# Own buffers for raw weights and adaLN tiles, a moved split at the mixer's start, and three merge buffers

## The chip, the cores and the metric

The kernel runs on one NeuronCore of a Trainium2 chip. The metric is the time of one execution on the device in microseconds. The names of the engines: PE is the matrix engine (TensorE), DVE the vector engine, ACT the scalar engine, POOL the GpSimd engine, SP the engine that issues most DMA transfers; "SPq" and "ACTq" are the rows of transfers issued by SP and ACT. Every engine works through its own instructions in the order in which they stand in the program and waits for the others by semaphores.

## What is computed

One layer of an encoder on a sequence of 512 tokens with 1024 channels, in float32:

```
mod = silu(c) @ w_ada + b_ada                  # 9 x 1024: shift, scale, gate of three blocks
h = h + 0.5 * g1 * FFN1(modulate(rmsnorm(h)))  # (silu(u @ Wa) * (u @ Wb)) @ w_down, inner size 2816
h = h +       g2 * Mixer(modulate(rmsnorm(h)))
h = h + 0.5 * g3 * FFN2(modulate(rmsnorm(h)))
out = rmsnorm(h)
```

The mixer multiplies by `w_in` (q, k, v, gates), runs a short convolution, a bidirectional chunked delta rule over 8 heads and a gated short-convolution branch. It projects both branches (`w_b_out` is the kernel's `w_bo`), merges them as sigmoid(gate_A)\*A + sigmoid(gate_B)\*B and multiplies by `w_out` (`w_o`). The adaLN product `silu(c) @ w_ada` is a matrix-vector product; its matrix has 72 tiles of 128 x 1024.

## The kernel before

**The products.** Activations lie transposed, channels on the 128 partitions and 512 tokens in the free dimension. A float32 product is made of three products of a reduced type: the weight is split into `hi` (a cast on ACT) and `lo` (a subtraction on DVE), the activation likewise into `uh`/`ul` or `g` hi/lo, and for each k-tile PE makes hi\*hi, lo\*hi and hi\*lo (lines 209, 210 and 211).

**A weight's way** (`weight`, lines 188 to 200). A raw tile of 128 x 1024 (512 KB; 128 x 768 for the third part of a down row) comes by one DMA from SP into the pool `wraw`, which has three buffers (L192). ACT casts it in halves of four k-tiles (L197), DVE subtracts (L199), and the halves lie in the pool `wsp` with three buffers for hi and three for lo. SP works in order: where a raw tile has no free buffer, SP stands, with all later transfers behind it. The scheduler gives the steps of a weight a priority that puts them ahead of their place in the code (`tc.high_priority(WOFF)`), and so orders each engine's instructions before the run.

**An adaLN tile** (`ada`, L172 and L173) is a raw tile of `w_ada` that DVE multiplies by the replicated activation and sums along the row; PE has no part in it. DVE works in order too: while it stands at an adaLN tile that has not arrived, the `lo` subtractions behind it wait. Tiles 0 to 15 come at the start, 16 to 31 during the last up products of FFN1, in buffers of `wraw`; 32 to 63 during FFN1's down product, in four slices of a tile named `room` that takes the place of FFN1's `uh`; and 64 to 71 during FFN2's down product, again in `wraw`. `spread` and `gate_along` hook them into the loops of products.

**The stages** (times of the profiled execution): start to 65 us; FFN1's up products to 251, with a fast form (fewer products, L406) from 107 to 206.5; FFN1's down product to 378, seven rows m of three weights each (the weight number n = 3m + i, 0 to 20) and the row m = 7 in two halves of 256 tokens; the mixer's projections and delta rule to 885; the merge to 930; `w_o` to 970; FFN2's up products to about 1205 and its down product to 1330.

**The mixer's start.** So that PE has work while FFN1's last half closes, the first three weights of `w_in`, numbers 12, 20 and 28, are split ahead into a pool `mlead` of six buffers, and are used in two halves of 256 tokens. `uh`(m) are the modulated inputs, made by ACT and DVE for each m and half. `sq` are the squares for the norm, `rs` the reciprocal root.

**The merge** (L1055 to 1080). For each of eight m, the gates' logits `msa` and `msb` and the first branch `mpa` come from DRAM by DMA from ACT's queue, ACT makes the sigmoids, DVE multiplies and adds, and the sum is split to `mh` and `ml`, the input of `w_o`. These tiles have two buffers each in the pool `mw`.

Of the kernel before, what the change touches and what calls it, by code (L numbers as in the profile page):

```python
# [16 lines left out]
P = 128  # L17
# [49 lines left out]
def tile_layer(  # L67
# [33 lines left out]
    wsp = open_pool(ctx, "wsp", bufs=3)  # L101
    upool = open_pool(ctx, "upool")
    sm = {}
    lead = {}
    psum = open_pool(ctx, "psum", bufs=ACC, space=PSUM)
    psx = open_pool(ctx, "psx", bufs=1, space=PSUM)
    psum_ch = open_pool(ctx, "psum_ch", bufs=CH, space=PSUM)
# [77 lines left out]
        dve.tensor_scalar(out=g, in0=g, scalar1=0.5, scalar2=None, op0=ALU.mult)  # L185


    def weight(src, nk, sp=None):
        sp = sp or wsp
        with tc.high_priority(WOFF):  # L190
            raw = wraw.tile([P, nk, P], F32, tag="raw", name="raw")
            nc.sync.dma_start(raw[:], src)  # L192
            parts = []
            for k in range(0, nk, 4):
                n = min(4, nk - k)
                hi = sp.tile([P, n, P], F32R, tag="hi", name="hi")
                act.copy(hi[:], raw[:, k : k + n, :])  # L197
                lo = sp.tile([P, n, P], F32R, tag="lo", name="lo")
                dve.tensor_sub(lo[:], raw[:, k : k + n, :], hi[:].bitcast(F32))  # L199
                parts.append((hi, lo))  # L200
        return parts
# [12 lines left out]
    def product(*args):  # L214
        for _ in product_steps(*args):
            pass
# [55 lines left out]

    HALVES = ((0, T // 2, "kq"), (T // 2, T, "o"))

    def residual(ws, rhs, gate, h, res, ssum, after, hp=0, tail=1, hook=None):

        def close(m, ps, r, t0, t1):
            dve.scalar_tensor_tensor(out=h[:, m, t0:t1], in0=ps[:, t0:t1], scalar=gate[:, m : m + 1],  # L280
                                     in1=r[:, t0:t1], op0=ALU.mult, op1=ALU.add)
            square_in(ssum, h[:, m, t0:t1], m, t0, t1)

        for m in range(KT - tail):
            ps, r = bank(), res(m)
            for i, (w, k0, nk, first, last) in enumerate(ws(m)):
                product(ps, weight(w, nk), rhs, k0, nk, first, last)
                if hook:
                    hook(3 * m + i)
# [22 lines left out]
    def ffn(st, u, big, hd, wu, wd, gate0, ssum, after, fast, early=None, hook=None, hook2=None, hp=0, base=0,  # L312
            up_done=None, comb=None, save=None):
        gp = open_pool(st, "gp")
        tp = open_pool(st, "ftp", bufs=2)
        T2 = T // 2
# [143 lines left out]
        for j in range(FT):  # L460
            if j == fast.start - 1:

                lead["st"].close()
                fp = open_pool(fst, "fast", side="right")
            if j == fast.start and full:
                put(0, x, *place[0])
            if j == fast.stop:
                part(4)
                fst.close()
                new_lead()  # L470
            if j in fast:
                i = 2 * j - ne + base
                split(hi[:, j, :], lo[:, j, :], seven(i, i + 1, fp)[:])
                continue
            ps = []
            for s in range(2):
                i = 2 * j + s - ne
                if i < 0:
                    ps.append(early[i])
                    continue  # L480
                ps.append(bank())
                product(ps[-1], weight(wu[i + base], KT), u, 0, KT, True, True)
                if hook:
                    hook(n)
                n += 1
            sa = tp.tile([P, T], F32, tag="sa", name="sa")
            act.activation(out=sa[:], in_=ps[0][:], func=ACT.Silu)
            dve.tensor_mul(sa[:], sa[:], ps[1][:])
            split(hi[:, j, :], lo[:, j, :], sa[:])
        if up_done:  # L490
            up_done()
        if full:
            fst.close()
            new_lead()
            ssum[:] = new_sums()
        h = big.tile([P, KT, T], F32, tag="big", name="h")

        def res(m):
# [2 lines left out]
            return r  # L501

        residual(lambda m: [(wd[m, :, k0 : k0 + nk, :], k0, nk, k0 == 0, k0 == 16) for k0, nk in ((0, 8), (8, 8), (16, 6))],
                 (hi, lo), mod[:, gate0 : gate0 + KT], h, res, ssum, lambda *t: after(h, *t), hp, hook=hook2)
        return h


    def mixer(st, u, h, post):
# [26 lines left out]
        with ExitStack() as dd:  # L535
# [14 lines left out]
            split(bw[:, :, 0:32], bw[:, :, 32:64], raw[:])  # L550
            sel = dt.tile([64, 32], F32, name="sel")
            dve.tensor_add(sel[:], ident[0:64, 0:32], ident[0:64, 32:64])
            lp = open_pool(dd, "mlead", bufs=6)
            ew = {i: weight(w_in[i], KT, lp) for i in (12, 20, 28)}
            ps = bank("ch", psum_ch)

            def early_half(t0, t1):
# [491 lines left out]
        with ExitStack() as mg:  # L1049
# [97 lines left out]
    csd = kept.tile([P, D], F32, name="csd")  # L1147
    h2d = kept.tile([P, KT, T], F32, name="h2d")

    def spread(a, b, j0, j1, then, bufs=None):  # L1150

        def hook(j):
            if j0 <= j < j1:
                for n in range(a + (b - a) * (j - j0) // (j1 - j0), a + (b - a) * (j + 1 - j0) // (j1 - j0)):
                    ada(n, raw=bufs and bufs[n % 4])
                    if n == 23:
                        modulation(16, 24)
                        mod_gate(0)
                if j == j1 - 1:
                    then()  # L1160
        return hook
# [4 lines left out]
        mod_scale(1)  # L1166
        mod_scale(2)

    u1 = u
    def room():  # L1170

        x = upool.tile([P, 4, D], F32, tag="uh", name="room")
        ada_bufs.extend(x[:, i, :] for i in range(4))
        u2.extend(new_u())

    u2, ada_bufs = [], []
    with ExitStack() as st:

        n = 2 * FAST1.start - E8
        h = ffn(st, u1, big, xT, w1u, w1d, 16, ssum, lambda h, *t: modulated(u2, h, 1, *t), FAST1, early,  # L1180
                spread(*ADA[0], n, 2 * (FT - len(FAST1)) - E8, lambda: None),
                spread(*ADA[1], 0, M1, mixer_ready, ada_bufs), up_done=room, comb=comb)
    lead["st"].close()
    first.close()
    with ExitStack() as st:
# [11 lines left out]
    with ExitStack() as st:  # L1197
# [78 lines left out]
```

## Time and profile before

| | us |
|---|---|
| median of 3 runs | 1346.35 (1344.49 to 1347.13) |
| profiled execution, its own time | 1341.37 |
| its span, first to last instruction | 1339.4 |
| PE busy | 1305.7 (97%) |
| DVE busy | 962.0 (72%) |
| ACT busy | 639.5 (48%) |
| granted clock, mean | 0.997 |

Lines of the profile read as follows. A group: line, engine, operation, out<-in, count, then busy time in us, the mean ns of one, and behind the bar the idle time before them with what ended most of it. A wait: engine and line, what it waited for, total us, times, the longest. A window: its stretch and length, busy us of PE, PEld, DVE, ACT and POOL (with counts), granted clock of PE (1.00 is full), share of the DMA engines, GB/s. A timeline row: start, duration, engine, line, operation; in brackets the idle time before and what ended it.

### The profile page before, as it was taken

How to read it: one execution, taken by the hardware profiler on the slowest of the kernel's cores; microseconds unless marked ns; L12 is line 12 of the kernel's file. 1: busy time of each engine (PE TensorE's matmuls, PEld its weight loads, DVE VectorE, ACT ScalarE, POOL GpSimd, SP SyncE). 2: the span in 40 equal slices, each digit the busy share in tenths (PEclk: the TensorE clock that was granted, in tenths of full speed). 3: DMA queues.
4: the chain of work that ended last, by engine and by line, in shares of the span. 5: the costliest groups of instructions: out<-in, count | busy, mean ns of one | idle time of the engine just before them, and what ended most of it. 6: DMA issues, size and time to landing. Idle time of an engine off the chain costs nothing.

```text
span 1339.4 us, 22097 instructions
## 1 busy us (share of the span) xinstructions
PE 1305.7 (97%) x8471; PEld 1132.9 (85%) x8471; DVE 962.0 (72%) x1983; ACT 639.5 (48%) x1299; POOL 64.6 (5%) x103
## 2 busy tenths in 40 slices
PE   8999999999999999999999999999999999999997
PEld 6889998777888888787777787887899999997886
DVE  7968887678367979776856784647688888884443
ACT  4445563222247773566464334545445556552230
POOL 0000000000010110112012001000000000000000
PEclk9999999999999999999999999999999999999999
DMA  9533336898433443344333242567523323335441
GB/s 349 173 110 111 111 124 205 286 339 286 143 130 104 149 147 118 100 139 130 111 111 117 73 142 80 187 198 245 187 111 110 111 95 109 112 116 169 140 127 63
DMA packets 83026, 199.91 MB, mean 149 GB/s; under 512 B 25129, under 2 KB 27369, under 8 KB 82666
## 3 DMA queue, kind: packets, MB, share of 16 engines
q1 hardware_dynamic: 64984, 164.29, 37.6%
q10 hardware_dynamic: 17938, 34.23, 7.4%
q8 instruction: 66, 1.08, 0.3%
q14 instruction: 38, 0.31, 0.1%
HBM read 175.39 MB, written 23.10 MB: 148 GB/s over the span
## 4 chain that ended last, share of the span: by engine, by line
PE 63%; DMA 12%; issue 10%; DVE 8%; ACT 4%; POOL 2%; SPq 0%; ACTq 0%; POOLq 0%; DVEq 0%
PE acc L406 11%; PE acc L211 11%; PE acc L210 10%; PE acc L209 10%; PE ch L406 8%; DMA room<-w_ada 3%; DVE lo L199 2%; DMA raw<-w_ada 2%; DMA msb<-gtd 2%; PE acc L1135 1%; ACT hi L197 1%; DMA raw<-w2u 1%; PE ch L872 1%; PE ch L1135 1%; PE o L895 1%
## 5 line engine op out<-in xcount | busy, mean ns | idle before, releaser
L197 ACT CAST hi<-raw 128x512 fp32r<-128x512 f32 (+1 forms) x304 | 181.7, 608 | 300.9 <-PE acc L211 245.0
L209 PE MATMUL acc<-uh,hi 128*128 128x512 f32 (+1 forms) x776 | 298.4, 386 | 3.8 <-ACT hi L197 2.3
L210 PE MATMUL acc<-uh,lo 128*128 128x512 f32 (+1 forms) x776 | 297.2, 384 | 0.4 <-DVE lo L199 0.3
L211 PE MATMUL acc<-ul,hi 128*128 128x512 f32 (+1 forms) x776 | 295.7, 383 | 0.0
L199 DVE TENSOR_TENSOR lo<-raw,hi 128x512 fp32r<-128x512 f32 (+1 forms) x304 | 202.5, 675 | 128.4 <-ACT hi L197 127.0
L209 PEld LDWEIGHTS acc<-uh,hi 128*128 128x128 f32 x776 | 146.9, 189 | 28.1 <-ACT hi L197 2.3
L210 PEld LDWEIGHTS acc<-uh,lo 128*128 128x128 f32 x776 | 146.8, 189 | 24.0 <-DVE lo L199 0.8
L211 PEld LDWEIGHTS acc<-ul,hi 128*128 128x128 f32 x776 | 146.2, 189 | 24.1
L210 PE MATMUL acc<-g,lo 128*128 128x512 f32 (+1 forms) x396 | 145.3, 367 | 3.4 <-DVE lo L199 3.4
L209 PE MATMUL acc<-g,hi 128*128 128x512 f32 (+1 forms) x396 | 145.1, 366 | 1.1 <-ACT hi L197 1.1
L211 PE MATMUL acc<-g,hi 128*128 128x512 f32 (+1 forms) x396 | 144.5, 365 | 0.0
L210 PEld LDWEIGHTS acc<-g,lo 128*128 128x128 f32 x396 | 74.4, 188 | 17.4 <-DVE lo L199 5.6
L209 PEld LDWEIGHTS acc<-g,hi 128*128 128x128 f32 x396 | 74.4, 188 | 13.6 <-ACT hi L197 1.5
L211 PEld LDWEIGHTS acc<-g,hi 128*128 128x128 f32 x396 | 74.4, 188 | 11.9
L406 PE MATMUL acc<-dh,hi 128*128 128x256 f32 x368 | 80.4, 282 | 0.2 <-ACT sa L414 0.2
L634 DVE SCALAR_TENSOR_TENSOR cacc<-acc,cvd_sb,cacc 128x510 f32<-128x510 f32 (+1 forms) x96 | 70.9, 742 | 3.2 <-ACT cacc L629 2.6
L220 DVE TENSOR_TENSOR lw<-raw,hw 128x1024 fp32r<-128x1024 f32 x42 | 51.4, 1224 | 28.8 <-ACT hw L219 28.2
L219 ACT CAST hi<-s 128x512 fp32r<-128x512 f32 x84 | 52.0, 620 | 36.5 <-PE ch L406 14.2
L219 ACT CAST hw<-raw 128x1024 fp32r<-128x1024 f32 x42 | 44.0, 1049 | 48.7 <-PE acc L406 27.7
L406 PE MATMUL acc<-dh,lo 128*128 128x256 f32 x224 | 63.3, 283 | 0.0
L406 PE MATMUL ch<-uh,lw 128*128 128x256 f32 x224 | 62.8, 280 | 0.0
L406 PE MATMUL ch<-ul,hw 128*128 128x256 f32 x224 | 62.8, 280 | 0.0
(378 smaller groups left out, 2771.2 us busy)
## 6 DMA issues: line engine op xcount, KB each, us to landing
raw<-w_in SPq DMA_DIRECT2D x60, 512.0 KB
raw<-w_ada SPq DMA_DIRECT2D x40, 512.0 KB
raw<-w2u SPq DMA_DIRECT2D x35, 512.0 KB
room<-w_ada SPq DMA_DIRECT2D x32, 512.0 KB
raw<-w1u SPq DMA_DIRECT2D x31, 512.0 KB
raw<-w1d SPq DMA_DIRECT2D x16, 512.0 KB
raw<-w2d SPq DMA_DIRECT2D x16, 512.0 KB
rb<-w2u SPq DMA_DIRECT2D x9, 512.0 KB
```

The source lines that it names most:

```text
L197: act.copy(hi[:], raw[:, k : k + n, :])
L199: dve.tensor_sub(lo[:], raw[:, k : k + n, :], hi[:].bitcast(F32))
L209: pe.matmul(ps[:, t0:t1], wh, rh[:, k0 + k, t0:t1], start=a, stop=False)
L210: pe.matmul(ps[:, t0:t1], wl, rh[:, k0 + k, t0:t1], start=False, stop=False)
L211: pe.matmul(ps[:, t0:t1], wh, rl[:, k0 + k, t0:t1], start=False, stop=b)
L219: act.copy(hi, src)
L220: dve.tensor_sub(lo, src, hi.bitcast(F32))
L406: pe.matmul(ps, a, b, start=first and k == 0 and a is wh and b is xh, stop=end, skip_group_check=not first)
L634: dve.scalar_tensor_tensor(out=acc[:, lo:hi], in0=src[:, lo + o : hi + o], scalar=w[:, i : i + 1], in1=acc[:, lo:hi], op0=ALU.mult, op1=AL ...
L872: pe.matmul(ps[:, 0:P], f[:, n, :], r, start=True, stop=True)
L895: pe.matmul(po[:, c * P : c * P + P], at[:, d, c, :], ys[d][c][:], start=d == 0, stop=d == 1)
L1135: pe.matmul(early[m][:], terms[i][0][:, m, :], terms[i][1], start=k == 0 and i == 0, stop=k == KT - 1 and i == 2)
```

## The change

Five edits, all on buffers:

1. `weight` can be given its raw tile. In a down product the weights with n > 2 and n % 7 < 4 (n = 3, 7, 8, 9, 10, 14, 15, 16, 17) land in slice n % 7 of the tile `y`, which has four slices of 128 x 1024 and lies in the place of the block's `ul`. The others stay in `wraw`.
2. The adaLN tiles 16 to 31 get a pool of their own with six buffers (`room["p"]`), in the space that the fast form's pool leaves; the pool `lead` is opened at the end of the up products instead.
3. All later adaLN tiles (32 to 63, and now 64 to 71 too) use the four slices in the place of `uh` (`room["x"]`).
4. At the mixer's start weight 12 is split into `wsp`; `mlead` has four buffers and holds 20 and 28.
5. The merge's pool `mw` has three buffers for each of its tiles.

```diff
-    def weight(src, nk, sp=None):
+    def weight(src, nk, sp=None, raw=None):
         sp = sp or wsp
         with tc.high_priority(WOFF):
-            raw = wraw.tile([P, nk, P], F32, tag="raw", name="raw")
+            if raw is None:
+                raw = wraw.tile([P, nk, P], F32, tag="raw", name="raw")
+            else:
+                raw = raw.rearrange("p (k x) -> p k x", x=P)[:, 0:nk, :]
...
-                product(ps, weight(w, nk), rhs, k0, nk, first, last)
+                n = 3 * m + i
+                product(ps, weight(w, nk, raw=raws and raws(n)), rhs, k0, nk, first, last)
...
             if j == fast.stop:
                 part(4)
                 fst.close()
-                new_lead()
+                room["p"] = open_pool(fst, "room", bufs=6, side="right")
...
-        if up_done:
-            up_done()
+        fst.close()
+        new_lead()
         if full:
-            fst.close()
-            new_lead()
             ssum[:] = new_sums()
+
+        x, y = (upool.tile([P, 4, D], F32, tag=tag, name="room") for tag in ("uh", "ul"))
+        room["x"] = [x[:, i, :] for i in range(4)]
...
-                 (hi, lo), mod[:, gate0 : gate0 + KT], h, res, ssum, lambda *t: after(h, *t), hp, hook=hook2)
+                 (hi, lo), mod[:, gate0 : gate0 + KT], h, res, ssum, lambda *t: after(h, *t), hp, hook=hook2,
+                 raws=lambda n: y[:, n % 7, :] if n > 2 and n % 7 < 4 else None)
...
-            lp = open_pool(dd, "mlead", bufs=6)
-            ew = {i: weight(w_in[i], KT, lp) for i in (12, 20, 28)}
+            lp = open_pool(dd, "mlead", bufs=4)
+            ew = {i: weight(w_in[i], KT, lp if i > 12 else wsp) for i in (12, 20, 28)}
...
-            mw = open_pool(mg, "mw", bufs=2)
+            mw = open_pool(mg, "mw", bufs=3)
...
-    def spread(a, b, j0, j1, then, bufs=None):
+    def spread(a, b, j0, j1, then):
...
-                    ada(n, raw=bufs and bufs[n % 4])
+                    if "x" in room:
+                        ada(n, raw=room["x"][n % 4])
+                    else:
+                        ada(n, room["p"])
...
-                ada(64 + j, cs=cs)
+                ada(64 + j, cs=cs, raw=room["x"][j % 4])
```

The line numbers of the kernel after are a few higher (L192 becomes L195, L197 L200, L199 L202, L580 L586). What moves on the engines is seen at three places.

SP, from the last up weights of FFN1 (`w1u`) into its down product (`w1d`); `w_ada` are the adaLN tiles. Before:

```order
L172 DMA raw<-w_ada 128x1024 x2
L192 DMA raw<-w1u 128x1024
L172 DMA raw<-w_ada 128x1024 x2
L192 DMA raw<-w1d 128x1024 x2
L192 DMA raw<-w1d 128x768
L192 DMA raw<-w1d 128x1024
L172 DMA room<-w_ada 128x1024 x3
```

and after the change:

```order
L195 DMA raw<-w1d 128x1024
L172 DMA raw<-w_ada 128x1024 x2
L195 DMA raw<-w1d 128x1024
L172 DMA raw<-w_ada 128x1024
L195 DMA raw<-w1d 128x768
L195 DMA raw<-w1d 128x1024
L195 DMA room<-w1d 128x1024 x2
L195 DMA room<-w1d 128x768
L195 DMA raw<-w1d 128x768
L195 DMA room<-w1d 128x1024
L172 DMA room<-w_ada 128x1024 x2
```

The first two down weights now stand before the last three of the adaLN tiles 16 to 31, and nine down weights instead of four stand before tile 32. These are n = 0, 1, 2, 4, then 3 and 7, 8, 5, 9.

DVE, at the same place (`g` is the last up product's result, `lo` a weight's half, L173 an adaLN tile). Before:

```order
L220 TENSOR_TENSOR g_2200<-sa,g_2200 128x512
L199 TENSOR_TENSOR lo<-raw,hi 128x512
L173 SCALAR_TENSOR_TENSOR room,part<-room,cs 128x1024 x2
L199 TENSOR_TENSOR lo<-raw,hi 128x512
L173 SCALAR_TENSOR_TENSOR room,part<-room,cs 128x1024
L199 TENSOR_TENSOR lo<-raw,hi 128x256
```

and after the change:

```order
L223 TENSOR_TENSOR g_2200<-sa,g_2200 128x512
L202 TENSOR_TENSOR lo<-raw,hi 128x512 x2
L202 TENSOR_TENSOR lo<-raw,hi 128x256
L173 SCALAR_TENSOR_TENSOR room,part<-room,cs 128x1024
L202 TENSOR_TENSOR lo<-room,hi 128x512
L173 SCALAR_TENSOR_TENSOR room,part<-room,cs 128x1024
L202 TENSOR_TENSOR lo<-room,hi 128x512
```

Tile 32 stood before the two halves of n = 2 and stands now behind them, before n = 3.

ACT, at the end of FFN1 and the mixer's start (`hi` is a cast of half a weight, `sq` and `uh` as above, the table load that of the exponential). Before:

```order
L197 CAST hi<-raw 128x512
L197 CAST hi<-raw 128x256
L229 ACTIVATE sq<-h 128x512
L229 ACTIVATE sq<-h 128x256
L269 ACTIVATE uh<-t,mod 128x256 x7
L580 ACT_TABLE_LOAD
L580 ACTIVATE nea<-hp_sb 128x16
L197 CAST hi<-raw 128x512 x6
L269 ACTIVATE uh<-t,mod 128x256
```

and after the change:

```order
L200 CAST hi<-raw 128x512
L200 CAST hi<-raw 128x256
L200 CAST hi<-raw 128x512 x2
L232 ACTIVATE sq<-h 128x512
L200 CAST hi<-raw 128x512
L232 ACTIVATE sq<-h 128x256
L272 ACTIVATE uh<-t,mod 128x256 x7
L586 ACT_TABLE_LOAD
L586 ACTIVATE nea<-hp_sb 128x16
L200 CAST hi<-raw 128x512 x4
L272 ACTIVATE uh<-t,mod 128x256
```

The two halves of weight 12, and the first of the next weight for the general buffers, are cast before the last squares; four casts are left behind the table load, where six stood.

More of the change, by code (lines that the diff above doesn't have):

```diff
@@ L103, in tile_layer @@
     sm = {}
-    lead = {}
+    lead, room = {}, {}
     psum = open_pool(ctx, "psum", bufs=ACC, space=PSUM)
@@ L273, in tile_layer, with residual @@
     HALVES = ((0, T // 2, "kq"), (T // 2, T, "o"))
-    def residual(ws, rhs, gate, h, res, ssum, after, hp=0, tail=1, hook=None):
+    def residual(ws, rhs, gate, h, res, ssum, after, hp=0, tail=1, hook=None, raws=None):
         def close(m, ps, r, t0, t1):
@@ L286, in residual @@
             for i, (w, k0, nk, first, last) in enumerate(ws(m)):
-                product(ps, weight(w, nk), rhs, k0, nk, first, last)
+                n = 3 * m + i
+                product(ps, weight(w, nk, raw=raws and raws(n)), rhs, k0, nk, first, last)
                 if hook:
-                    hook(3 * m + i)
+                    hook(n)
             close(m, ps, r, 0, T)
@@ L312, in ffn @@
     def ffn(st, u, big, hd, wu, wd, gate0, ssum, after, fast, early=None, hook=None, hook2=None, hp=0, base=0,
-            up_done=None, comb=None, save=None):
+            comb=None, save=None):
         gp = open_pool(st, "gp")
@@ L1167, in mixer_ready, with next_u @@
         mod_scale(2)
[L1169 to L1176, printed above, removed]
+    def next_u(h, t0, t1, bc):
+        if t0 == 0:
+            u2.extend(new_u())
+        modulated(u2, h, 1, t0, t1, bc)
+    u1, u2 = u, []
     with ExitStack() as st:
         n = 2 * FAST1.start - E8
-        h = ffn(st, u1, big, xT, w1u, w1d, 16, ssum, lambda h, *t: modulated(u2, h, 1, *t), FAST1, early,
+        h = ffn(st, u1, big, xT, w1u, w1d, 16, ssum, next_u, FAST1, early,
                 spread(*ADA[0], n, 2 * (FT - len(FAST1)) - E8, lambda: None),
-                spread(*ADA[1], 0, M1, mixer_ready, ada_bufs), up_done=room, comb=comb)
+                spread(*ADA[1], 0, M1, mixer_ready), comb=comb)
     lead["st"].close()
```

## The prediction

> **What bounds the kernel now.** I read the page's busy shares first, then its groups of instructions, then for each stage the waits of PE, and last the windows around the waits.
>
> ```profile
> PE 1305.7 (97%) x8471; PEld 1132.9 (85%) x8471; DVE 962.0 (72%) x1983; ACT 639.5 (48%) x1299; POOL 64.6 (5%) x103
> L209 PE MATMUL acc<-uh,hi 128*128 128x512 f32 (+1 forms) x776 | 298.4, 386 | 3.8 <-ACT hi L197 2.3
> L210 PE MATMUL acc<-g,lo 128*128 128x512 f32 (+1 forms) x396 | 145.3, 367 | 3.4 <-DVE lo L199 3.4
> L209 PE MATMUL acc<-g,hi 128*128 128x512 f32 (+1 forms) x396 | 145.1, 366 | 1.1 <-ACT hi L197 1.1
> ```
>
> PE is busy 97% of the span, and the matmuls' number is not touched. So the change can win only the time in which PE stands, and that is small: each of these groups idled 1 to 4 us in the whole run. The releasers named are ACT's casts and DVE's subtractions, which split a raw weight into hi and lo. I looked at each place by itself.
>
> The start of the mixer (waits and windows; the last columns of a window are granted clock, DMA share, GB/s):
>
> ```profile
> PE acc L209 <- ACT hi L197: 2.3, 1, 2.3
> PE acc L209 <- DVE sps L587: 0.9, 1, 0.9
> 378.62 1.28 ACT L580 ACT_TABLE_LOAD   x1
> 380.03 2.16 ACT L197 CAST hi<-raw 128x512 fp32r<-128x512 f32 x4
> 380.69 0.39 PE L209 MATMUL acc<-uh,hi 128*128 128x256 f32 x1 [2.25 <-ACT hi L197]
> 381.42 0.58 PE L210 MATMUL acc<-uh,lo 128*128 128x256 f32 x1 [0.34 <-DVE lo L199]
> 378.00:380.00 2.00, 0.43 (x5) 0.35 (x3) 1.33 (x5) 1.88 (x3) 1.57 (x4) 1.00 0.00 0
> 380.00:382.00 2.00, 0.97 (x3) 0.77 (x4) 1.33 (x3) 2.00 (x5) 0.35 (x1) 0.85 0.61 262
> 382.00:384.00 2.00, 2.00 (x11) 2.00 (x11) 2.00 (x4) 1.96 (x5) 0.00 (x0) 0.50 1.06 442
> 384.00:386.00 2.00, 2.00 (x17) 2.00 (x16) 0.76 (x2) 0.00 (x0) 0.00 (x0) 0.80 1.20 344
> ```
>
> The mixer's first product needs w_in[12] split. Its cast stands on ACT behind a table load, so PE idles 2.25 us, then 0.34. The granted clock is 0.85, 0.50 and 0.80 in the three windows behind the gap.
>
> FFN1's down product (251 to 378):
>
> ```profile
> PE acc L209 <- ACT hi L197: 3.4, 2, 2.3
> PE acc L210 <- DVE lo L199: 2.2, 5, 1.1
> DVE room L173 <- DMA room<-w_ada: 16.7, 13, 2.5
> SPq L192 <- DVE raw L173: 16.2, 6, 4.1
> 245.96 3.44 SPq L192 DMA_DIRECT2D raw<-w1d  x3
> 248.00:252.00 4.00, 3.36 (x15) 2.44 (x13) 1.05 (x2) 0.19 (x1) 0.00 (x0) 1.00 0.96 343
> 252.00:256.00 4.00, 3.29 (x13) 2.53 (x14) 3.18 (x5) 2.19 (x4) 0.00 (x0) 1.00 0.45 114
> 255.00:265.00 10.00, 10.00 (x46) 8.28 (x45) 6.02 (x10) 2.28 (x5) 0.00 (x0) 1.00 0.98 372
> 285.00:295.00 10.00, 10.00 (x46) 8.29 (x45) 9.69 (x19) 2.70 (x5) 0.00 (x0) 1.00 0.95 334
> 296.00:300.00 4.00, 2.88 (x13) 2.10 (x12) 2.36 (x4) 1.24 (x2) 0.00 (x0) 1.00 0.90 282
> 312.00:316.00 4.00, 3.73 (x17) 2.77 (x16) 2.84 (x4) 1.24 (x2) 0.00 (x0) 1.00 0.94 306
> 328.00:332.00 4.00, 3.79 (x17) 2.84 (x16) 3.27 (x8) 1.24 (x2) 0.00 (x0) 1.00 0.39 140
> ```
>
> Two causes. At 251 the first down weight is late: SP issued it only at 245.96, because it stood at a slot of `wraw` that an adaLN tile held (16.2 us in six such waits). Later DVE, which works in order, stands at an adaLN tile still under way (16.7 us, 13 times), and the subtractions behind it come late. The DMA engines are nearly full there, share 0.95 to 0.98.
>
> The merge and FFN2's down product:
>
> ```profile
> PE acc L209 <- ACT mh L219: 1.4, 1, 1.4
> 929.55 0.63 ACT L1064 ACTIVATE msa<-msa 128x512 f32<-128x512 f32 x1 [1.30 <-DMA msa<-gtd]
> 924.96 0.33 ACTq L1063 DMA_DIRECT2D msa<-gtd  x1
> 933.47 0.50 PE L209 MATMUL acc<-mh,hi 128*128 128x512 f32 x1 [1.35 <-ACT mh L219]
> PE acc L210 <- DVE lo L199: 1.6, 1, 1.6
> 1231.99 0.33 SPq L172 DMA_DIRECT2D raw<-w_ada  x1
> 1237.43 1.22 DVE L173 SCALAR_TENSOR_TENSOR raw<-raw,cs 128x1024 f32<-128x1024 f32 x1 [4.47 <-DMA raw<-w_ada]
> 1236.00:1240.00 4.00, 2.43 (x11) 1.72 (x10) 2.57 (x5) 0.00 (x0) 0.00 (x0) 1.00 0.14 19
> ```
>
> In the merge the last `msa` was issued late and everything up to `mh` hung on it. In FFN2, DVE stood 4.47 us at an adaLN tile that shares `wraw`.
>
> **How a gap is counted.** The records give a 512-column matmul 0.39 us:
>
> ```profile
> 296.89 0.39 PE L210 MATMUL acc<-g,lo 128*128 128x512 f32 x1
> 297.12 0.39 PE L211 MATMUL acc<-g,hi 128*128 128x512 f32 x1
> ```
>
> but one starts every 0.23 us. A gap therefore costs its idle time plus 0.39 - 0.23 = 0.16 us of lost overlap. A down weight has 8, 8 or 6 k-tiles of three matmuls, on average 22 x 0.23 = 5.0 us of PE.
>
> **The change part by part.** No matmul, cast, subtraction or DMA is added or taken away; only orders and waits change.
>
> *Start of FFN1's down.* Idle is 4.00 - 3.36 = 0.64 and 4.00 - 3.29 = 0.71 us in the two windows, 1.35 us in two gaps; with the overlap 1.35 + 2 x 0.16 = 1.7 us. The adaLN tiles 16 to 31 now have six buffers of their own, so the weights stop queuing behind them, and in the new order SP issues the first two `w1d` before the last three `w_ada` of that stage. The six waits of 16.2 us on SP go. An issue at least 5 us sooner covers 1.1 us of lateness. Gain 1.7 (bounds 0 and 1.7). What is added: these tiles wait for the space that the pool of the fast loop leaves, and start three weights later; their users (the gate) come only at the first closing of the down product, some 15 us after 251.
>
> *Inside FFN1's down.* Three gaps: 1.12, 0.27 and 0.21 us of idle, plus 3 x 0.16: 2.1 us. Nine weights now go to space left by `ul`, so up to four more are on their way. That is not free. The windows show the DMA engines full, and a 512 KB tile takes 0.524 MB / 0.36 MB per us = 1.5 us there. Three weights brought forward push every later adaLN tile back by 4.4 us. DVE in the new order takes the first of them one weight later, 5.0 us. The slack is thus 0.6 us, about nothing: the large gap may go, the small ones stay or move. I take a gain of 0.8, between 2.1 (all gaps gone) and -2.0 (they double), nearer to the rows of before because bytes and engines are the same.
>
> *Mixer start.* w_in[12] now goes to the general buffers `wsp`. In the new order its two casts stand before the last squares of FFN1, so ahead of the table load. Gone: 2.25 + 0.16 = 2.4 us. The clock: 2 us at 0.50 lose 1.0, 2 us at 0.80 lose 0.4, and half of 2 us at 0.85 lose 0.2: 1.6 us, which I expect to go with the gap. Left: w_in[20] is cast behind the table load as before, from 380.03, and its lo comes at about 381.4, while PE has 7 of 8 k-tiles of w_in[12] (21 x 0.12 = 2.5 us from 378.4, to 380.9) until then: a gap of 0.5 us instead of 0.34 + 0.16; and the last k-tile waits for `uh`, which ACT makes behind four casts (380.03 + 4 x 0.55 = 382.2, then 0.5), so 0.5 more. Gain 2.4 + 1.6 - 0.5 = 3.5 (bounds 1.9 if the clock falls all the same, 4.5 if nothing new waits). `mlead` with four buffers holds w_in[20] and [28] just as before; w_in[12] takes two of three general buffers, and w_in[36] behind it waits until PE is through with it, which is at most 3 us and covered by the products of 20 and 28 (2 x 24 x 0.12 = 5.8 us).
>
> [...]
>
> *Merge.* Three buffers instead of two let the transfers of step 7 start when step 4 is through instead of step 5. Neighbouring `msa` issues:
>
> ```profile
> 921.29 0.33 ACTq L1063 DMA_DIRECT2D msa<-gtd  x1
> ```
>
> so the step is 924.96 - 921.29 = 3.7 us, and 929.55 becomes about 926. The chain moves by more than PE's 1.35 us. Gain 1.35 + 0.16 = 1.5 (bounds 0 and 1.9).
>
> *FFN2's down.* The tiles 64 to 71 go to `uh`'s space, and weights no longer stand between them. The order has at most four on their way. Idle in the window is 1.57 us in one gap: 1.57 + 0.16 = 1.7, and with the small waits at the end of the up products 1.9. What speaks against: the first tile cannot start before the last matmul that reads the space,
>
> ```profile
> 1203.17 0.28 PE L406 MATMUL ch<-ul,hw 128*128 128x256 f32 x1
> ```
>
> so at 1203, where before it had long been under way; but no DMA crowd is there (share 0.14), and 1.5 us a tile is well under 5.0 us a weight. Gain 1.9 (bounds 0 and 2.3).
>
> *Not touched:* the wait at 407 for DVE's `sps` (0.9 us). PE comes there 3.5 us earlier; DVE's work ahead of it hangs on the same products and moves along. I count nothing, and up to 3.5 us of loss in a rival.
>
> **The sum.** 1.7 + 0.8 + 3.5 + 1.5 + 1.9 = 9.4 us. The profiled execution took 1341.37 us (span 1339.4): 1341.37 - 9.4 = 1332.0. The median of the runs, 1346.35, lies 5.0 above that execution, so the forecast is **1337.0 us**. All upper bounds: 1.7 + 2.1 + 4.5 + 1.9 + 2.3 = 12.5, so 1333.9.
>
> **Rivals.**
>
> *Half of it comes back.* The wait at 407 takes the mixer's 3.5 us, since DVE's and ACT's own work from 380 on (ACT is full, 2.00 and 1.96, in the windows) and not PE sets it, and the DVE queue keeps its gaps in FFN1. Left: 1.7 + 1.5 + 1.9 = 5.1 us, so 1341.3. For it: ACT and DVE are dense there. Against it: 0.9 us is all that PE waits now.
>
> *Nothing measurable.* If SP's earlier issues only fill queues that are full already (0.95 to 0.98) and FFN2's tiles, now starting at 1203, make the same gap again, only the merge stays, 1.5 us: 1344.9. Against it: at 1237 the share is 0.14, so that tile was late for its slot, not for bandwidth.
>
> *Slower.* DVE in order behind adaLN tiles, in FFN1's down. Five weights now go ahead of tile 32 in SP's order that went behind it: 5 x 1.5 = 7.5 us. If DVE stands 7 us at two places (weights 6 and 10, where the slack above is least): in before a DVE wait of 2.50 us
>
> ```profile
> 297.64 1.23 DVE L173 SCALAR_TENSOR_TENSOR room<-room,cs 128x1024 f32<-128x1024 f32 x1 [2.50 <-DMA room<-w_ada]
> ```
>
> cost PE 1.12 + 0.16 = 1.3, so 1.2 is covered, and each such wait would cost 7 - 1.2 = 5.8, and 1.6 of clock as at the mixer: 14.8 for two. Less the 2.1 that this replaces and the other gains (8.6): 4.1 slower, 1350.5. It decides from 2 x (w - 1.2 + 1.6) = 10.7, w = 5.0 us each. Against it: the tiles have four slots, and DVE takes them a weight later too.
>
> **How the numbers follow.** Forecast 0.58, half comes back 0.26, nothing 0.10, slower 0.06. What a measurement of this kernel can tell from no change is about 0.2%, 2.7 us: below 1343.7 is faster, above 1349.0 slower. The first two cases are faster: 0.84; same 0.10; slower 0.06. The range holds the first two with their bounds, 1332 to 1344; the upper bounds' 1333.9 with 2 us of a median's own spread give the lower end.
>
> **What would show it.** Right: no wait of PE above 1 us at 251, 298, 378, 932 and 1237; granted clock 1.00 from 378 to 390; the first w1d issued before 240; SP's waits at L192 for L173 gone; DVE's waits for `w_ada` in FFN1's down not above 17 us in total and none over 3 us; in FFN2 none over 1 us. Wrong: a clock of 0.50 without a gap before it; a wait at 407 of 3 us or more; DVE waits for `room` of 5 us, with PE gaps behind them; a new long wait of ACT for `w_in` before 378.

## The result and the profile after

The changed kernel takes 1334.3 us (median of 4 runs, 1334.0 to 1335.76), the kernel before beside it 1345.59 (4 runs). The ratio is 0.9927, with a 95% interval of 0.9900 to 0.9953. The forecast was 1337.0, the range 1332 to 1344. With more runs in a later comparison (9 against 32, below) the ratio is 0.9950 (0.9933 to 0.9967), 6.7 us. The runs of one kernel spread by more than any one of the gaps that the change works on: before lay between 1337.78 and 1346.63 us in those 32 runs.

The page after, its span and first group (the same columns as before):

```profile
span 1333.8 us, 22069 instructions
PE 1306.3 (98%) x8471; PEld 1134.3 (85%) x8471; DVE 961.6 (72%) x1983; ACT 640.5 (48%) x1299; POOL 64.6 (5%) x103
```

The work is the same. PE's busy time is that of before within 0.6 us; the span is 5.6 us shorter, so PE stands less.

The start of the mixer after, waits and windows:

```profile
PE acc L212 <- DVE sps L593: 0.5, 1, 0.5
381.05 0.39 PE L213 MATMUL acc<-uh,lo 128*128 128x256 f32 x1 [0.32 <-DVE lo L202]
384.64 0.71 PE L259 MATMUL o<-ident,rs 128*128 128x128 f32 x4 [0.30 <-POOL rs L256]
378.00:380.00 2.00, 2.00 (x18) 2.00 (x19) 0.96 (x4) 1.97 (x4) 1.92 (x4) 1.00 0.00 0
380.00:382.00 2.00, 1.68 (x15) 1.48 (x14) 1.70 (x3) 2.00 (x5) 0.00 (x0) 1.00 0.94 393
382.00:384.00 2.00, 2.00 (x20) 2.00 (x19) 1.36 (x4) 0.56 (x2) 0.11 (x1) 1.00 0.93 393
384.00:386.00 2.00, 1.70 (x14) 1.50 (x14) 0.61 (x2) 0.09 (x1) 0.59 (x1) 1.00 1.03 274
```

The 2.25 us wait for the cast is gone, two waits of 0.3 us are left, and the granted clock stays at 1.00. The wait for `sps` did not grow (0.9 before, 0.5 now).

FFN1's down product after: SP's first `w1d`, the windows, and DVE's waits for the adaLN tiles.

```profile
236.41 0.33 SPq L195 DMA_DIRECT2D raw<-w1d  x1
246.00:256.00 10.00, 10.00 (x46) 8.29 (x45) 5.38 (x10) 3.42 (x6) 0.00 (x0) 1.00 0.55 164
295.00:305.00 10.00, 10.00 (x45) 8.26 (x44) 8.73 (x15) 3.01 (x5) 0.00 (x0) 1.00 0.97 354
315.00:325.00 10.00, 9.22 (x42) 7.31 (x40) 6.38 (x12) 2.80 (x5) 0.00 (x0) 1.00 0.92 320
325.00:335.00 10.00, 9.06 (x39) 7.15 (x40) 9.23 (x16) 1.86 (x4) 0.00 (x0) 1.00 0.73 235
DVE room L173 <- DMA room<-w_ada: 16.3, 11, 3.6
323.03 1.23 DVE L173 SCALAR_TENSOR_TENSOR room<-room,cs 128x1024 f32<-128x1024 f32 x1 [3.62 <-DMA room<-w_ada]
```

The first weight comes 9.6 us earlier and PE is busy throughout 246 to 256. The gap that stood at 298 is gone too, but two others came, at 324 and 330 (9.22 and 9.06 of 10 us busy). DVE waits 16.3 us for adaLN tiles, where it waited 16.7.

The merge and FFN2's down product after:

```profile
924.26 0.63 ACT L1070 ACTIVATE msa<-msa 128x512 f32<-128x512 f32 x1 [1.02 <-DMA msa<-gtd]
926.83 0.63 ACT L1076 ACTIVATE msb<-msb 128x512 f32<-128x512 f32 x1 [0.91 <-DMA msb<-gtd]
926.19 0.69 DVE L1073 TENSOR_TENSOR msa<-msa,mpa 128x512 f32<-128x512 f32 x1 [1.51 <-DMA mpa<-pad]
930.59 0.50 PE L212 MATMUL acc<-mh,hi 128*128 128x512 f32 x1 [0.93 <-ACT mh L222]
DVE room L173 <- DMA room<-w_ada: 7.5, 5, 3.9
1228.00:1236.00 8.00, 8.00 (x37) 6.64 (x36) 5.42 (x10) 2.50 (x4) 0.00 (x0) 1.00 0.53 166
```

`msa` comes 5.3 us earlier than before (924.26 against 929.55). Of these, 2.5 us are only the earlier stages' gain: the matmul that PE starts at 926.05 before, it starts at 923.59 now. Against that matmul `msa` moved by 2.8 us. Yet PE still waits 0.93 us for `mh`: now DVE stands for `mpa` until 926.19 and has work without a break from there to 929.89. `msb`, on which ACT starts at 926.83, arrives later still, but DVE is not free for it before 928.00. In FFN2, DVE still waits for tiles, up to 3.9 us at once, but PE no longer waits.

### The profile page after: what moved, and what is told of

Its sections match the earlier page's. It is cut to its first block, busy times and chain, and to the rows that moved or that the text cites. A ratio compares the mean times of both kernels' runs of the same rounds, so it can differ in the third digit from the quotient of the medians.

```text
span 1333.8 us, 22069 instructions
## 1 busy us (share of the span) xinstructions
PE 1306.3 (98%) x8471; PEld 1134.3 (85%) x8471; DVE 961.6 (72%) x1983; ACT 640.5 (48%) x1299; POOL 64.6 (5%) x103
## 4 chain that ended last, share of the span: by engine, by line
PE 68%; issue 10%; DMA 9%; DVE 7%; ACT 4%; POOL 2%; SPq 0%; ACTq 0%; POOLq 0%; DVEq 0%
PE acc L214 12%; PE acc L213 11%; PE acc L212 11%; PE acc L410 11%; PE ch L410 8%; DMA room<-w_ada 2%; DVE lo L202 2%; PE acc L1141 1%; DMA msa<-gtd 1%; DVE room L173 1%; DMA msb<-gtd 1%; ACT hi L200 1%; PE ch L878 1%; PE ch L1141 1%; PE o L901 1%
## 5 line engine op out<-in xcount | busy, mean ns | idle before, releaser
L200 ACT CAST hi<-raw 128x512 fp32r<-128x512 f32 (+1 forms) x268 | 161.5, 611 | 257.7 <-PE acc L214 210.7
L202 DVE TENSOR_TENSOR lo<-raw,hi 128x512 fp32r<-128x512 f32 (+1 forms) x268 | 180.2, 681 | 108.2 <-ACT hi L200 106.7
L213 PEld LDWEIGHTS acc<-g,lo 128*128 128x128 f32 x396 | 74.4, 188 | 15.5 <-DVE lo L202 3.4
L173 DVE SCALAR_TENSOR_TENSOR room<-room,cs 128x1024 f32<-128x1024 f32 x40 | 48.8, 1223 | 24.0 <-DMA room<-w_ada 23.8
L410 PE MATMUL ch<-uh,hw 128*128 128x256 f32 x224 | 62.9, 281 | 0.0
```

The lines of the kernel that those rows point to most:

```text
L173: dve.scalar_tensor_tensor(out=raw, in0=raw, scalar=1.0, in1=cs[:], op0=ALU.mult, op1=ALU.mult, accum_out=part[:, n : n + 1])
L213: pe.matmul(ps[:, t0:t1], wl, rh[:, k0 + k, t0:t1], start=False, stop=False)
L410: pe.matmul(ps, a, b, start=first and k == 0 and a is wh and b is xh, stop=end, skip_group_check=not first)
```

## The experiments

Two ways of reading are used. The *time* is a ratio of the kernel's runs to those of before beside it, with its interval; it is not the quotient of the two medians that are given with it, and differs from that by up to 0.0011. In five rounds it cannot tell less than about 2.3 us. The *stage difference* compares two profiled executions: the same matmul, counted in PE's order, is looked up in both traces at the stage's borders, and the stage's length is subtracted. Its borders in the first profile of before are 0, 30, 245, 257, 374, 392, 560, 885, 926, 940, 1185, 1250 and the end. These are the differences in us to that first profile, taken between the starts of these matmuls; "all" goes to the start of the last one, and the stages between the columns, with differences of up to 1.5 us, are left out:

```
                        0-30   245-257  257-374  374-392  560-885  926-940  1185-1250  all
after                   +1.7    -1.9     +0.1     -3.7     +1.7     -0.4      -2.2     -5.6
after, again            +2.2    -1.9     -0.4     -3.8     +2.3     -0.3      -2.5     -5.1
before, again           +2.9    +2.4     -1.1     -1.4     +1.3     -0.2      -0.7     +3.6
mixer's edit alone      +2.9    -0.3     -1.1     -3.8      0.0     -1.0      -1.6     -5.6
gap filled              +2.0    +2.9     +0.9     -0.5     +1.3     +0.3      -2.2     +4.8
merge's edit alone      +0.5    -0.4     -0.3     +1.1     +2.1     +0.2      +2.1     +5.8
buffers alone           +2.7    -1.9     -0.7     -0.2     -0.7     -1.0      -2.3     -4.9
no weights in y         +1.1    -1.9     +0.4     -3.8     +1.2     -0.5      -2.5     -6.7
four tiles earlier       0.0    -1.9     -0.7     -3.8     -0.6     -0.3      -2.5    -10.9
tiles from POOL         +1.9    -1.9    +15.5     -3.7     +0.3     -0.2      +5.3    +16.9
four merge buffers      +1.6    -1.9     -1.1     -3.7     +0.6     -0.5      -2.3     -8.2
tiles and mixer alone   +2.6    -1.9     -0.3     -3.7     +0.2     -1.1      -2.5     -6.4
earlier and four        +1.8    -1.9     +0.7     -3.7     +1.0     -0.3      -2.0     -6.1
```

The columns 0-30 and 560-885 are not touched by any edit; they differ by up to 3 us between executions. This is why a time here needs many runs, and why the first profiles differ by 5.6 us only.

Much of this is the granted clock. After, and then "four tiles earlier":

```profile
19.75 1.15 PE L1141 MATMUL acc<-uh,wfh 128*128 128x512 f32 x3 [1.81 <-ACT wfh L1125]
20.00:22.00 2.00, 2.00 (x7) 1.53 (x7) 2.00 (x3) 1.42 (x2) 0.00 (x0) 0.59 1.02 416
22.00:24.00 2.00, 2.00 (x7) 1.59 (x6) 2.00 (x5) 0.23 (x1) 0.00 (x0) 0.55 1.03 406
561.73 0.49 PE L743 MATMUL o<-kT 128*128 128x128 f32 x2 [1.21 <-DVE at L752]
562.00:564.00 2.00, 2.00 (x25) 1.81 (x25) 1.94 (x10) 0.66 (x2) 0.00 (x0) 0.77 0.03 8
564.00:566.00 2.00, 2.00 (x11) 2.00 (x11) 1.49 (x6) 0.97 (x4) 0.00 (x0) 0.50 0.00 0
566.00:568.00 2.00, 2.00 (x16) 1.95 (x15) 1.30 (x5) 1.85 (x7) 0.41 (x1) 0.87 0.49 193
19.60 0.96 PE L1141 MATMUL acc<-uh,wfh 128*128 128x512 f32 x3 [1.81 <-ACT wfh L1125]
20.00:22.00 2.00, 2.00 (x10) 1.63 (x9) 2.00 (x3) 1.57 (x2) 0.00 (x0) 1.00 1.03 418
```

The gap of 1.81 us near 20 us stands in all 14 profiles. Behind it the clock fell to about half in nine, with the stage 0-30 at +1.7 to +2.9, and stayed up in five (the first profile of before among them), with 0.0 to +1.6. A gap of 1.2 or 1.6 us near 565 us stands in all 14 too; behind it the clock fell in six, with the stage 560-885 at +1.0 to +2.3, and stayed up in eight, with -0.7 to +1.3. The places that the change works on behave alike. Behind gaps of 1.83 us (before, again) and 2.65 us (gap filled) near 256 us, and of 2.25 us at 1243 us (merge's edit alone), the clock fell too; the longer gaps and the falls together make the +2.4, +2.9 and +2.1 of the table:

```profile
256.40 0.49 PE L209 MATMUL acc<-g,hi 128*128 128x512 f32 x1 [1.83 <-ACT hi L197]
258.00:260.00 2.00, 2.00 (x6) 1.54 (x5) 1.56 (x3) 0.62 (x1) 0.00 (x0) 0.50 0.67 150
1243.11 0.50 PE L210 MATMUL acc<-g,lo 128*128 128x512 f32 x1 [2.25 <-DVE lo L199]
1244.00:1246.00 2.00, 2.00 (x8) 1.52 (x7) 1.52 (x5) 1.14 (x2) 0.00 (x0) 0.62 0.97 374
```

### Before, once more

The kernel is unchanged.

> The kernel before, unchanged, profiled once more. The medians moved by 11.3 us, the two profiled executions only by 5.6 us (1341.37 to 1335.76). Theory A, the profiled execution of before was a lucky one: this profile takes 1344 to 1347 us, and the extra 3 to 5 us show as longer PE gaps at places where the change works (251, 298, 378, 932, 1237) or in the delta rule. Theory B, the two executions are typical and the medians differ by something a profile does not show: this profile takes 1341 to 1342 us while its timed runs stay at 1345 to 1347.

The profiled execution took 1344.93 us, the 12 runs had a median of 1344.76, and 35 runs of before on that chip 1342.83 (1337.93 to 1347.94). The time is that of theory A, but its account holds in part only: 1341.37 was an ordinary execution, and so were the 1344 to 1347 of the first few runs. The 3.6 us that it took longer lie in the first 30 us (+2.9), at the start of the down product (+2.4) and in the delta rule (+1.3), less 1.4 at the mixer, 1.1 inside the down product and 0.7 in FFN2. At the mixer this is what happened, with the same wait as in the first profile:

```profile
385.17 0.38 PE L209 MATMUL acc<-uh,hi 128*128 128x256 f32 x1 [2.39 <-ACT hi L197]
383.90:385.90 2.00, 0.39 (x2) 0.19 (x2) 0.75 (x2) 1.99 (x5) 0.80 (x2) 1.00 0.31 131
385.90:387.90 2.00, 2.00 (x17) 2.00 (x18) 2.00 (x4) 2.00 (x5) 0.00 (x0) 1.00 1.13 475
387.90:389.90 2.00, 2.00 (x20) 2.00 (x19) 1.50 (x4) 0.54 (x2) 0.22 (x1) 1.00 1.16 385
```

A gap of 2.39 us, and the clock stays at 1.00. So the half clock of the first profile does not follow every such gap.

### The mixer's edit alone

```diff
-            lp = open_pool(dd, "mlead", bufs=6)
-            ew = {i: weight(w_in[i], KT, lp) for i in (12, 20, 28)}
+            lp = open_pool(dd, "mlead", bufs=4)
+            ew = {i: weight(w_in[i], KT, lp if i > 12 else wsp) for i in (12, 20, 28)}
```

> Before with edit 4 alone (weight 12 split into wsp, mlead of four). Theory: the 2.25 us wait of PE at 378 and the windows of clock 0.85, 0.50 and 0.80 behind it go, the matmul that waits at 407 comes 3.5 to 4 us earlier, and the whole takes 3 to 4 us less than before (ratio 0.997 to 0.998). Rival, it comes back: the wait at 407 for DVE's sps grows from 0.9 to 3 us or more and the whole moves by less than 1 us.

1341.24 against 1342.83 us, ratio 0.9986 (0.9968 to 1.0004). That alone tells neither from no change. In the profile the stage is 3.8 us shorter, the clock 1.00, the wait at 407 does not grow, and the difference between the whole change (0.9950) and the buffers alone (0.9975, below) is 3.4 us. The theory holds in the traces; its size in the time, 1.6 to 3.4 us, is within the uncertainty of both.

### The mixer's gap filled

```diff
+            idle_work(18)
             for t0, t1 in ((0, T // 2), (T // 2, T)):
```

> Before with 18 small matmuls on constants (about 2.25 us by the 18 rows of them at the start of the profile of before) put on PE in front of the mixer's first product, where PE idled 2.25 us; nothing else is changed and the cast of weight 12 stays behind the table load. Theory, the gap itself lowers the clock: the windows from 380 to 386 show 1.00 instead of 0.85, 0.50, 0.80, and the kernel is 1.3 to 2 us faster though no wait is removed. [...]

```profile
384.26 4.26 PE L116 MATMUL acc<-ones,ident 128*128 128x128 f32 x36
386.00:388.00 2.00, 2.00 (x20) 2.00 (x19) 1.22 (x3) 1.99 (x6) 0.32 (x1) 1.00 0.63 262
388.00:390.00 2.00, 2.00 (x19) 2.00 (x18) 2.00 (x5) 2.00 (x5) 0.00 (x0) 1.00 0.94 393
```

The 18 small matmuls left 36 records here, so the filling took 4.26 us, twice what was meant, 1.9 us more than a gap of 2.39. The clock stayed at 1.00, which alone shows little, since it did so behind the open gap above too. The time, 1343.63 against 1342.83 (1.0004, 0.9986 to 1.0023), tells nothing, as it must with 1.9 us added where 1.6 may be saved. What the clock does is read best over all profiles: of four with the gap left open, three show a fall (first profile, merge's edit alone, buffers alone) and one does not (before, again); of ten with the gap gone (nine) or filled (one) none does. The merge's profile has the deepest:

```profile
381.29 0.58 PE L209 MATMUL acc<-uh,hi 128*128 128x256 f32 x1 [2.38 <-ACT hi L197]
380.60:382.60 2.00, 1.16 (x3) 0.87 (x4) 1.33 (x3) 2.00 (x5) 0.23 (x1) 0.58 0.61 262
382.60:384.60 2.00, 2.00 (x11) 2.00 (x11) 2.00 (x4) 1.96 (x5) 0.00 (x0) 0.50 1.06 442
384.60:386.60 2.00, 2.00 (x11) 2.00 (x11) 0.77 (x2) 0.00 (x0) 0.00 (x0) 0.50 1.20 344
386.60:388.60 2.00, 2.00 (x15) 2.00 (x14) 0.16 (x1) 0.00 (x0) 0.23 (x1) 0.71 0.72 291
```

In these windows, as (1 - clock) x 2 us, 0.8 + 1.0 + 1.0 + 0.6 = 3.4 us are lost to the clock behind a gap of 2.38 us (the 0.8 in a window in which PE stood until 381.29), and none behind 2.39 us above. At this place the clock fell only where the gap was open; what decides whether it then falls is not shown.

### The merge's edit alone

```diff
-            mw = open_pool(mg, "mw", bufs=2)
+            mw = open_pool(mg, "mw", bufs=3)
```

> Before with edit 5 alone (mw of three buffers). After the whole change PE still waited 0.93 us for mh at 930.6, where it had waited 1.35. Theory as seen there: msa comes earlier but mpa takes its place as the last transfer (DVE L1073 waits for mpa 1.5 us), so this gains 0.4 us, not 1.5: no measurable change. Rival, the wait at 930 in the whole change is due to the other edits' traffic: alone it gains 1.5 us and the wait at 932 goes.

1344.1 against 1342.83 us, ratio 1.0010 (0.9994 to 1.0025): no gain. Its stage is +0.2 us, and PE still waits 0.9 us for `mh`, so the other edits' traffic is not the cause. Over all profiles, the merge stage is 0.0, -0.2, -1.0, +0.3, -1.0 and -1.1 with two buffers, and -0.4, -0.3, +0.2, -0.5, -0.3 and -0.2 with three: no shorter. With two buffers the wait for `mh` is anything from 0.2 to 1.7 us; with three it is 0.8 to 0.9 each time.

### After, once more

The kernel is unchanged.

> The changed kernel unchanged, with more rounds. Runs of before on this chip spread from 1337.9 to 1347.9 us (35 runs, median 1342.8), and the first comparison had four of each. By the stages of the profiles, the gaps of PE before sum up to about 9 us over those after (start of the down product 2 to 3, mixer 2.4 to 4, merge 0.4, FFN2 1.9). Theory, all of it holds on average: ratio 0.993 to 0.995. Rival, the 11.3 us of the first medians were right: 0.991 to 0.992. Other rival, half of it was chance: 0.996 or more.

1334.14 against 1342.07 us, ratio 0.9950 (0.9933 to 0.9967). That is 6.7 us by the ratio and 7.9 by the medians: the first theory, at its lower end; the interval reaches into the range of the other rival too (0.996 or more). The 11.3 us of the first comparison are too much, since its four runs of before lay in the upper half of what the kernel takes here; whether that was chance or the chip is not shown.

### The buffers alone

```diff
-            ew = {i: weight(w_in[i], KT, lp if i > 12 else wsp) for i in (12, 20, 28)}
+            ew = {i: weight(w_in[i], KT, lp) for i in (12, 20, 28)}
...
-            mw = open_pool(mg, "mw", bufs=3)
+            mw = open_pool(mg, "mw", bufs=2)
```

(and `mlead` with six buffers again.)

> The change without the mixer's and the merge's edits: the buffers of weights and adaLN tiles alone (edits 1 to 3). Theory: no PE wait at 251 and 1237, the mixer's 2.3 us wait back at 378; 4 to 5 us faster than before (ratio 0.9965). Rival: the gaps inside FFN1's down take the gain back (as the profile after shows 1.6 us of new waits at 324 and 330): 2 us or less.

1338.28 against 1342.07 us, ratio 0.9975 (0.9956 to 0.9994), 3.4 us, between the sizes of theory and rival. The start of the down product is 1.9 us and FFN2's stage 2.3 us shorter. The mixer's gap is back, 2.32 us, and the clock behind it falls to 0.63 and 0.52:

```profile
380.46 0.55 PE L212 MATMUL acc<-uh,hi 128*128 128x256 f32 x1 [2.32 <-ACT hi L200]
380.00:382.00 2.00, 1.37 (x5) 1.07 (x6) 1.56 (x3) 2.00 (x5) 0.07 (x1) 0.63 0.91 385
382.00:384.00 2.00, 2.00 (x11) 2.00 (x11) 2.00 (x4) 1.73 (x4) 0.00 (x0) 0.52 0.95 401
```

### No weights in `y`

```diff
-                 raws=lambda n: y[:, n % 7, :] if n > 2 and n % 7 < 4 else None)
+                 raws=None)
```

> After, with all down weights in wraw again (edit 1 undone; the adaLN tiles keep their own buffers). DVE's order then has tile 32 before n = 2 as in before. Theory, the gain at 251 and 1237 is due to the adaLN tiles' own buffers, and the weights' extra places only push the tiles back on full DMA engines: no PE wait at 251 and 1237, and inside FFN1's down waits of 1 to 3 us, as before; the same as after within 1 us. Rival, the weights' places carry the gain: PE waits above 1 us come back at 251 or 1237 and it is 2 to 4 us slower than after.

1334.63 against 1342.07 us, ratio 0.9954 (0.9937 to 0.9970): that of after. No wait of PE at 251, none in FFN2's down product, and inside FFN1's down product four small ones, one of them at the mixer:

```profile
PE acc L213 <- DVE lo L202: 2.0, 4, 1.2
```

The theory holds. The adaLN tiles' own buffers carry the gain at 251 and 1237; nine weights in the room of `ul` bring nothing that can be measured, and lose nothing.

### Four tiles earlier

```diff
-ADA, M1 = ((16, 32), (32, 64)), 20
+ADA, M1 = ((16, 36), (36, 64)), 20
```

> After, with adaLN tiles 32 to 35 moved from FFN1's down product to its last up products (20 tiles there instead of 16, 28 instead of 32). Theory, the waits left at 324 and 330 come from too many bytes between 255 and 325: 2.1 MB less there, 6 us of DMA, and both waits go, 1.6 us faster than after. Rival, the up stage is as full (share 0.87 to 0.97 from 216 to 246), the first down weights come late and a wait of 1 us or more shows at 251; or the last tiles, which SP issues only behind a weight that waits for its slot, stay late: no gain.

1335.85 against 1342.07 us, ratio 0.9954 (0.9936 to 0.9972): no gain over after. The profiled execution was the shortest of all, 1330.44 us, but by the table this comes mostly from the columns that no edit touches (0.0 and -0.6, where after has 1.7 and 1.7): its clock did not fall there. Inside the down product, one wait of 1.3 us and 14.2 us of DVE's waits stay. No wait appears at 251. Fewer bytes did not remove the last wait; the rival's second half, that SP's order keeps the last tiles late, is neither refuted nor shown.

### The tiles issued by POOL

```diff
-        nc.sync.dma_start(raw, w_ada[n])
+        (nc.sync if n < 16 else nc.gpsimd).dma_start(raw, w_ada[n])
```

> After, with the transfers of the adaLN tiles 16 to 71 issued by POOL instead of SP; slots, bytes and DVE's order stay. In after, SP stood 128 us at weights that waited for a slot (SPq L195 for DVE L202), with tiles behind them, and PE lost 1.6 us at 324 and 330. Theory, the tiles are late because of SP's order: issued as soon as their slot is free, DVE's waits for w_ada in FFN1's down fall from 16 us to under 8 and the last PE gaps there go; 1.5 us faster than after. Rival, the DMA engines' bandwidth sets it (share 0.92 to 1.02): the tiles only take it from the weights, DVE's waits stay at 14 to 17 us or turn into late weights, PE waits of 1 to 2 us stay; no gain.

1358.09 against 1341.58 us, ratio 1.0114 (1.0092 to 1.0136): 16.5 us slower, which neither expected. PE's waits from 200 to 340 us, DVE's, and two windows:

```profile
PE acc L213 <- DVE lo L202: 11.1, 5, 3.6
DVE room L173 <- DMA room<-w_ada: 21.3, 14, 4.5
265.00:275.00 10.00, 6.37 (x24) 4.53 (x23) 7.53 (x13) 1.24 (x2) 2.69 (x5) 0.91 0.97 364
285.00:295.00 10.00, 7.38 (x30) 5.75 (x29) 6.72 (x13) 1.86 (x3) 2.69 (x5) 0.93 0.96 364
```

One premise failed: DVE's order did not stay. With the tiles off SP's queue the scheduler put them earlier on DVE, two in front of many a `lo` where after has one. The DMA engines were full as before (0.97), and the 32 tiles still took 259.53 to 327.95 us to go through DVE, 68 us against 71 us in after (265.46 to 336.61). But more of them stood ahead of each weight, and PE waited for `lo`, five times, 11.1 us, and ran at a lower clock in between (0.91 and 0.93 here). In FFN2, whose tiles POOL issues too, PE waited another 5.2 us for `lo`, and that stage is 5.3 us longer. This is the path of the prediction's slower rival, brought about by another edit: DVE waits up to 4.5 us at one tile, and the stage is 15.5 us longer. The edit changed the issuer and DVE's order at once, so that the order is the cause is likely but not shown; POOL's issues under an unchanged order were not tried.

### Four buffers in the merge

```diff
-            mw = open_pool(mg, "mw", bufs=3)
+            mw = open_pool(mg, "mw", bufs=4)
```

> After, with four buffers in the merge instead of three. In the profiles with three buffers the merge stage was no shorter than in those with two (excess over the first profile -0.3 to -0.45 against -1.0 to 0.3 us), since mpa arrives last. Theory, transfers that are issued still earlier only queue behind the weights of w_bo and w_o on the same DMA engines: PE still waits 0.5 to 1 us for mh. Rival, one more step of lead hides it: no PE wait for mh, 1 us less in that stage. The whole cannot tell 1 us.

1333.01 against 1341.58 us, ratio 0.9928 (0.9905 to 0.9951), not told apart from after. PE still waits 0.8 us for `mh`, the stage is 0.1 us shorter than in after. The theory holds: a buffer more is not what the last step lacks.

### The tiles and the mixer alone

```diff
-                 raws=lambda n: y[:, n % 7, :] if n > 2 and n % 7 < 4 else None)
+                 raws=None)
...
-            mw = open_pool(mg, "mw", bufs=3)
+            mw = open_pool(mg, "mw", bufs=2)
```

> After without edit 1 (no weights in y) and without edit 5 (two merge buffers): the adaLN tiles' own buffers and the mixer's split alone. Theory, these two carry the whole gain: ratio 0.993 to 0.996, no measurable difference from after; no PE wait at 251, 378 and 1237. Rival, the small parts add up: 2 us or more slower than after.

1334.35 against 1341.99 us, ratio 0.9935 (0.9917 to 0.9953). PE's waits in FFN1's down product and in the merge (window 915 to 940), with two merge buffers:

```profile
PE acc L213 <- DVE lo L202: 1.1, 2, 0.7
PE acc L212 <- ACT mh L222: 0.2, 1, 0.2
```

The gain, as far as these intervals tell, is all here without the weights in `y` and without the third merge buffer. In this execution the merge's wait is even the shortest of all.

### Four tiles earlier and four merge buffers

Both edits above together.

> After with tiles 32 to 35 in the up stage and four merge buffers together. Each alone showed ratios of 0.9954 and 0.9928 against 0.995 of after. Theory: no better than after by more than 1.5 us, 0.993 to 0.995, with one wait of 1.3 us left in FFN1's down and 0.8 us in the merge. Rival, the two add up: 0.992 or less.

1336.71 against 1341.99 us, ratio 0.9967 (0.9951 to 0.9983): no better than after, and short of the 0.993 to 0.995 of the theory. More waits are left than it said, 2.7 us in two inside the down product and 0.9 us in the merge. No version beat the changed kernel by more than these intervals tell.

## Why the prediction was right, step by step

**The start of the down product**: 1.7 us forecast, 1.9 us in every one of the nine profiles with the tiles' own buffers that stand in the table. The mechanism was the one named: SP issued the first `w1d` at 236.41. With the old buffers this stage varies from execution to execution (0.0, +2.4, -0.3, +2.9 and -0.4 us in five profiles), so on their mean of +0.9 the gain is 2.8. The term left out that the clock falls behind this gap in some executions (two of the five).

**Inside the down product**: 0.8 us forecast, about nothing measured. After is +0.1 and -0.4 us; the profiles with the old buffers scatter from -1.1 to +0.9. The step that failed is "the large gap may go, the small ones stay or move": the large gap went, and gaps of the same sum came elsewhere, while DVE waits as long (16.3 us against 16.7). That the full DMA engines keep it so was argued, not shown: the runs did not separate their rate from SP's order. The bound of zero was nearer than the value taken.

**The mixer's start**: 3.5 us forecast, 3.7 measured against the first profile. The parts hold: the 2.25 us went, 0.32 and 0.30 stayed where 0.5 and 0.5 were expected, the clock stayed up. The term of the clock, 1.6 us, is a mean at best: 0, 1.7, 1.7 and 3.4 us, over whole windows, in the four profiles with the gap open.

**The merge**: 1.5 us forecast, 0.4 in the profile and none by the experiments. The step that failed is "the chain moves by more than PE's 1.35 us". `msa` did move, by 2.8 us against PE (3.5 were forecast), but I had looked at one of three transfers; DVE then stood for `mpa`, 1.9 us behind `msa`, and on DVE the rest of the chain stands among `lo` subtractions (from 926.19 to the cast at 929.9). Nor was the 1.35 us a fixed size: with two buffers it is 0.2 to 1.7 us.

**FFN2's down product**: 1.9 us forecast, 2.2 measured against the first profile. Here too the old buffers' gap varies (0.0, -0.7, -1.6, -2.2 and +2.1 us, a mean of -0.5), while with the tiles' own buffers, issued by SP, the stage is at -2.0 to -2.5 each time. But DVE's waits, which were to be under 1 us, are 7.5 us in five. They no longer reach PE.

**The rivals**: the wait at 407 stayed small (0.5 us), so the mixer's gain was not given back; the tiles behind a full DMA did not stall DVE for 5 us (longest 3.6). That 3.6 is over the 3 us, and FFN2's 3.9 over the 1 us, that the prediction named as bounds if it was right: of its signs these two did not come.

**The time**: the terms as measured add up to 1.9 - 0.1 + 3.7 + 0.4 + 2.2 = 8.1 us, against 9.4 forecast, and the runs show 6.7 (4.4 to 9.0). Means over the profiles with and without each edit give 2.8, 0.0, 3.6, -0.2 and 1.9, the same 8.1. So the 9.4 is above this interval, and the 5.1 of "half of it comes back" lies inside it, though by no path that this rival named. The last step, "lies 5.0 above that execution", was wrong too: the profiled execution was an ordinary one, and the median of three runs was high. Over 32 runs before has 1342.07, just 0.7 above that execution; 1342.07 - 9.4 would have been 1332.7, and after's nine runs beside them have 1334.14. A base that was 4.3 us too high and a gain that was too large partly cancelled: that 1337.0 came as near as 2.7 us is in part luck.

## What to carry to other kernels

Give a stream that one engine consumes in order buffers of its own, before giving the bulk stream more: here the adaLN tiles' buffers took two stalls of about 2 us away, and nine more weight places nothing. Before adding a buffer, name the transfer that will be last once this one is early. In the stage whose DMA engines were nearly full (0.92 to 0.97), extra lead moved a gap here and did not close it.

Before reading a change of a few us, profile the unchanged kernel twice: stages that no edit touches differed by up to 3 us here. Read the granted clock behind each gap of PE before giving such a difference to an edit.

## What the runs showed of the hardware that was not expected

Behind one and the same gap of PE the clock fell to about half in some executions and not in others: behind 2.3 to 2.4 us at the mixer in three profiles of four (lowest windows of 2 us 0.50, 0.50 and 0.52), behind 1.81 us near 20 us in nine of 14 (0.55 in after), behind 1.2 or 1.6 us near 565 us in six of 14 (0.50 in after). Summed over windows of 2 us as (1 - clock) x 2 us, a fall took 1.7 us in each of four cases (after near 20 us and behind 562 us, the first profile and "buffers alone" at the mixer) and 3.4 us in a fifth (the merge's edit alone, at the mixer).

The start of the execution, up to 30 us, took up to 2.9 us longer in one execution than in another of the same kernel; a fall like the one in after (0.59 and 0.55 in two windows) makes 1.7 us.

The 18 float32 matmuls of 128 columns that filled the mixer's gap left 36 records in 4.26 us, one every 0.12 us.
